# Moving the adaLN modulation sums of a two-layer decoder kernel: from among the routing scores into the pair stage and the last third of routing

## The chip, the cores and the metric

The kernel runs on one core of a Trainium2 chip. The core has five engines, each with an instruction queue of its own: TensorE (PE, with its weight loads as PEld), VectorE (DVE), ScalarE (ACT), GpSimd (POOL) and SyncE (SP), which issues most of the DMA transfers. The metric is the device time of one execution in microseconds; the median of several runs is compared.

## The reference

Two layers work on 512 tokens of width 1024. What matters here is cut out below; `rwkv7_mix` is the recurrent mixer of 8 heads, and the expert layer picks, for each token and head, 16 of 16384 experts by the sums of two 128-way scores.

```python
c_act = jax.nn.silu(c)
for l in range(DEPTH):
    mod = c_act @ ada_w[l] + ada_b[l]                 # 1024 x 6144, one row
    sh1, sc1, g1, sh2, sc2, g2 = jnp.split(mod, 6, axis=-1)
    h = modulate(rmsnorm(x, ln1_g[l]), sh1, sc1)
    ...
    x = x + g1[:, None, :] * mix
    h2 = modulate(rmsnorm(x, ln2_g[l]), sh2, sc2)
    x = x + g2[:, None, :] * peer_ffn(h2, peer_q[l], peer_keys[l], peer_u[l], peer_v[l])
return rmsnorm(x, lnf_g)
```

## The kernel before, in words

The 6144 modulation columns of a layer are done in 12 groups of 512. The groups 0 and 1 are the first shift, 2 and 3 the first scale, 4 and 5 the first gate, 6 and 7 the second shift, 8 and 9 the second scale, 10 and 11 the second gate. A group is a weighted sum of eight 128x512 tiles: `ada_acc` loads them and makes one DVE `tensor_scalar` and seven DVE `scalar_tensor_tensor` on an accumulator `acc`; `ada_mod` then adds up its 128 rows with four one-column matmuls and adds the bias with one small DVE operation. With `early=True` a group is loaded by eight transfers of 256 KB into the general ring `s2` (38 slots), else by four of 512 KB into the ring `raw` (three slots), which the weight loads use as well.

Each layer is a mixer and an expert layer (`peer`).

- **Mixer.** After the input projection the eight heads go in four pairs through blocks (`blocks`, 20 each), a chain of 15 chunk steps (`chain`: a PE product `psc`, then two small DVE operations that give the next state `M`) and an output part. `zipped` deals the blocks of one pair, the chain of the pair before and the output of the one before that evenly; the list `ada` is dealt with them, a third of its entries (`len(ada) // 3`) in each of the first two of these rounds and the rest in the third. Entry i does `ada_mod` of group i-1 and `ada_acc` of group i of `ADA_MIX`. Six groups (4 to 9) give seven entries, so two, two and three.
- **Scoring.** In `peer`, 16 query projections (`project_q`, 24 matmuls each) alternate with `score`: eight matmuls, then `top16` on DVE for four token tiles. From the second projection on, every second one also starts a group of `ADA_PRE` (six in layer 0, two in layer 1), and `ada_mod` comes four projections later.
- **Routing.** A list `main` of weighted steps is dealt by `blend` with the 88 chunks (`s_ahead`, 24 matmuls of 384 columns) whose activations are spilled to memory: first the last score and the picks of token tile 0, then the picks of tile 1, then for t = 1, 2, 3 sixteen `onehot` steps each (four DVE operations, sixteen matmuls), with the picks of tile t+1 between them for t = 1 and 2. The weights (WO = 2.4 for a `onehot`, WP = 2.8 for a pick, and so on) set how many chunks each part gets: `at` splits the 88 chunks over the three parts. Each chunk needs a weight tile split into two halves by ACT (L259) and DVE (L260).
- **Dense.** The 128 chunks are then multiplied by the gates and by the value rows.

The text of the program is in the order told above, and a planner then orders each engine's queue by a simulated timeline. `tc.issue_after(ins)` holds what is traced in its block, on the engine of `ins` alone, behind `ins` in the queue.

Of the kernel before, what the change touches and what calls it, by code (L numbers as in the profile page):

```python
# [15 lines left out]
ALU = mybir.AluOpType  # L16
# [5 lines left out]
NT = T // P  # L22
D = 1024
ND = D // P
L = 2
# [9 lines left out]
SPILL = 88  # L35
GPRE = 24
GFRAC = 0.0
ADA_MIX = [[(l, g) for g in range(4, 10)] for l in range(L)]
ADA_PRE = [[(0, 10), (0, 11), (1, 0), (1, 1), (1, 2), (1, 3)], [(1, 10), (1, 11)]]
ADA_DENSE = [[], []]  # L40
SIDES, NPRE = (0, 8, 0, 3), 2
APER, AOFF, ADEL = 2, 1, 4
# [66 lines left out]
def body(ctx, tc, A, tap=None):  # L109
    nc = tc.nc  # L110
    V, S, G, TE = nc.vector, nc.scalar, nc.gpsimd, nc.tensor
# [11 lines left out]
    def nm(p):  # L123
        cnt[0] += 1
        return f"{p}{cnt[0]}"
# [3 lines left out]
    def bank(shape=(P, T)):  # L129
        return psp[0].tile(list(shape), F32, tag="ps", name=nm("ps"))  # L130

    def sbank(shape=(P, T)):
        return pss.tile(list(shape), F32, tag="pss", name=nm("pss"))

    def s2t(name, shape=(P, T), dt=F32):
        return s2.tile(list(shape), dt, tag="s2", name=nm(name))
# [6 lines left out]
    sc_ = pers.tile([P, ND], F32, name="silu_c")  # L143
# [5 lines left out]
    def C(n):  # L149
        o, w = COFF[n]  # L150
        return const[:, o:o + w]
# [21 lines left out]
    A2 = [pers.tile([P, ND], F32, name=f"A2_{l}") for l in range(L)]  # L173

    first = {}

    def ada_acc(l, g, side=0, early=False):
        acc = s2t("acc")
# [23 lines left out]
    def ada_mod(l, g, acc):  # L202
        pt = sbank((P, 4))
        for m in range(4):
            TE.matmul(pt[:, m:m + 1], acc[:, m * P:(m + 1) * P], C("one"), start=True, stop=True)
        o = VOFF["adab"][0]
        V.tensor_tensor(mods[l][:, 4 * g:4 * g + 4], pt, vecs[l][:, o + 4 * g:o + 4 * g + 4], op=ALU.add)
        if g in (2, 3, 8, 9):
            mod_scale(l, 1 if g < 6 else 2, g % 2)
# [25 lines left out]
    def mod_scale(l, which, half):  # L235
        a, ln, off = (A1, "ln1", 8) if which == 1 else (A2, "ln2", 32)
        o = 4 * half
        V.scalar_tensor_tensor(a[l][:, o:o + 4], mods[l][:, off + o:off + o + 4], 1.0, vec(l, ln, o, 4), op0=ALU.add, op1=ALU.mult)
# [79 lines left out]
    def mixer(l):  # L318
        with ExitStack() as mctx:
# [433 lines left out]

            todo, accs = ADA_MIX[l], {}

# [61 lines left out]
    def peer(l):  # L817
        with ExitStack() as pctx:
# [34 lines left out]
            pace, adas = {}, []  # L853
# [38 lines left out]
            with ExitStack() as rctx:  # L892
# [124 lines left out]
                def onehot(b):  # L1017
                    if not ohr:
                        ohr.extend([[s2t("oh", (P, TB // 2, NK, 2), F16) for _ in range(4)] for _ in range(3)])
                    oj, oi, x1, x2 = ohr[b % 3]  # L1020
                    every = iot.unsqueeze(1).to_broadcast([P, TB // 2, NK, 2])

                    def bc(n):
                        z = sel[n][:, b * TB:(b + 1) * TB].rearrange("p (a b) -> p a b", b=2)
                        return z.unsqueeze(2).to_broadcast([P, TB // 2, NK, 2])

                    V.tensor_tensor(oi, every, bc("i"), op=ALU.is_equal)
                    V.tensor_tensor(x1, oi, bc("g1"), op=ALU.mult)  # L1028
                    V.tensor_tensor(x2, oi, bc("g2"), op=ALU.mult)  # L1029
                    pace["V"] = V.tensor_tensor(oj, every, bc("j"), op=ALU.is_equal)  # L1030
                    onehot_mm()
                    pend.append(b)
# [19 lines left out]

                pre = list(ADA_PRE[l])
                for hp in range(16):
# [13 lines left out]
                def steps(t):  # L1068
                    a, b = route(t)
                    return [(WC, a[0])] + [(WP, f) for f in a[1:-1]] + [(WG, a[-1]), (WT, b)]  # L1070

                steps0 = [(WP, score)] + steps(0)
                steps1 = steps(1)
                main = steps0 + steps1
                for t in range(1, NT):
                    oh = [(WO, lambda b=b: onehot(b)) for b in range((t - 1) * P // TB, t * P // TB)]
                    nx = steps(t + 1) if t + 1 < NT else []
                    for i in range(len(oh)):
                        main.append(oh[i])
                        if nx:  # L1080
                            main.append(nx.pop(0))
                    main += nx
# [18 lines left out]
                w = T // (IG * GB)  # L1101
# [9 lines left out]
            acc = [[bank() for _ in range(2)] for _ in range(NTD)]  # L1111
# [147 lines left out]
    for l in range(L):  # L1259
        mixer(l)  # L1260
        peer(l)
# [56 lines left out]
```

## Time and profile before

| | us |
|---|---|
| median of 3 runs | 3419.54 |
| lowest and highest of them | 3406.15, 3427.21 |
| the profiled execution, its own time | 3418.91 |
| its span in the trace | 3417.1 |

The mean granted TensorE clock of the profiled execution was 0.956 of full speed. In the trace layer 0 has its pair stage at about 230 to 380 us, scoring at 430 to 558, routing at 558 to 985; layer 1 at about 1930 to 2070, 2119 to 2230 and 2230 to 2657. "PE" is matmul time, and a row "a <-b" names who ended a wait. Busy time counts an instruction from its start to its end, so pipelined instructions overlap a little.

### The profile page before, as it was taken

The numbers are of one execution on the slowest core, as the hardware profiler recorded it, in microseconds if no ns is written. First come the engines' busy times: TensorE is split into PE (matmuls) and PEld (weight loads), VectorE is DVE, ScalarE is ACT, GpSimd is POOL, SyncE is SP. The second block draws the span as 40 slices with busy tenths as digits, with TensorE's granted clock in tenths as the row PEclk, the third lists the DMA queues.
The fourth block names the chain that finished last, engine by engine and source line by source line (L and its number), as shares of the span: only waits on it lengthen the run. The fifth ranks groups of instructions, "written<-read, shape, count | busy, mean of one in ns | idle before, by whom it ended". The sixth has DMA issues, their size and how long they took to land. (4 is left out here: it accounts for less than half of the span.)

```text
span 3417.1 us, 52040 instructions
## 1 busy us (share of the span) xinstructions
PE 3187.3 (93%) x18634; PEld 2786.5 (82%) x18634; DVE 2787.6 (82%) x6195; ACT 1396.2 (41%) x2260; POOL 867.6 (25%) x684
## 2 busy tenths in 40 slices
PE   5989898999999999999899898999999999999997
PEld 3777678999998888888777776889999888888886
DVE  5677599989878888899938665999898688888998
ACT  3443222456553343333353433334556433333333
POOL 2000002332212222555400000033240122245664
PEclk7989899999999999999989888999999999999999
DMA  5214343577799999999922233346777999999996
GB/s 197 78 56 153 105 162 122 167 246 258 247 332 348 346 349 315 371 379 371 348 84 81 81 112 124 99 145 197 257 240 278 330 334 343 342 343 345 356 383 251
DMA packets 361380, 826.47 MB, mean 242 GB/s; under 512 B 46496, under 2 KB 189600, under 8 KB 357792
## 3 DMA queue, kind: packets, MB, share of 16 engines
q1 hardware_dynamic: 287392, 554.68, 48.3%
q0 software_dynamic: 73728, 268.47, 20.9%
q8 instruction: 146, 2.39, 0.3%
q14 instruction: 114, 0.93, 0.1%
HBM read 730.75 MB, written 92.27 MB: 241 GB/s over the span
## 5 line engine op out<-in xcount | busy, mean ns | idle before, releaser
L277 PE MATMUL pss<-hi,wsp 128*128 128x384 f32 (+1 forms) x5168 | 1079.9, 360 | 93.0 <-DVE wsp L260 29.1
L1165 PE MATMUL ps<-vv,wg 128*128 128x512 f32 x4608 | 1077.3, 392 | 26.4 <-ACT vv L1148 13.0
L277 PEld LDWEIGHTS pss<-hi,wsp 128*128 128x128 f32 x5168 | 940.0, 195 | 167.7 <-DVE wsp L260 40.2
L1165 PEld LDWEIGHTS ps<-vv,wg 128*128 128x128 f32 x4608 | 867.0, 189 | 210.6 <-ACT vv L1148 17.9
L259 ACT ACTIVATE wsp<-raw 128x1024 fp32r<-128x1024 f32 x341 | 359.9, 1057 | 571.0 <-PE pss L277 403.0
L277 PE MATMUL pss<-lo,wsp 128*128 128x384 f32 (+1 forms) x2584 | 535.3, 347 | 0.0
L858 POOL DMA_INDIRECT row<-u,ex x256 | 313.8, 1226 | 844.1 <-DVE row L864 644.4
L260 DVE TENSOR_TENSOR wsp<-raw,wsp 128x1024 fp32r<-128x1024 f32 x341 | 430.9, 1264 | 76.1 <-ACT wsp L259 75.6
L277 PEld LDWEIGHTS pss<-lo,wsp 128*128 128x128 f32 x2584 | 462.3, 189 | 22.5 <-issue 0.5
L858 POOL DMA_INDIRECT row<-v,ex x256 | 333.6, 1303 | 252.5 <-DVE ox L872 202.9
L1149 DVE TENSOR_TENSOR vv<-raw,vv 128x512 fp32r<-128x512 f32 x512 | 344.2, 689 | 48.8 <-ACT vv L1148 44.1
L1148 ACT ACTIVATE vv<-raw 128x512 fp32r<-128x512 f32 x512 | 291.5, 618 | 120.6 <-DMA raw<-v 83.3
L864 DVE SCALAR_TENSOR_TENSOR row<-row,hx 128x1024 f32<-128x1024 f32 x256 | 318.3, 1249 | 13.3 <-DMA row<-u,ex 13.3
L872 DVE SCALAR_TENSOR_TENSOR ox<-row,wx,ox 128x1024 f32<-128x1024 f32 x254 | 325.2, 1280 | 2.4
L1139 ACT ACTIVATE wg<-ge 128x384 fp32r<-128x384 f32 x256 | 133.0, 524 | 472.4 <-DVE ge L1137 177.2
L974 POOL TENSOR_TENSOR eq<-eq,cid 128x400 f32<-128x400 f32 x128 | 181.7, 1439 | 481.2 <-DVE eq L972 343.0
L940 POOL TENSOR_TENSOR hf<-hi,lo 128x128 f32<-128x128 f32 x16 | 8.1, 526 | 894.8 <-DVE tw L909 868.0
L1140 DVE TENSOR_TENSOR wg<-ge,wg 128x384 fp32r<-128x384 f32 x256 | 141.2, 555 | 108.2 <-ACT wg L1139 97.3
L1049 ACT ACTIVATE gb<-ps 128x512 f32<-128x512 f32 x192 | 199.2, 1163 | 0.0
L1137 DVE TENSOR_TENSOR ge<-ge,g 128x192 f32<-128x192 f32 x496 | 156.8, 353 | 37.1 <-DMA g<-gscr 23.6
L1132 ACT ACTIVATE ge<-pss 128x384 f32<-128x384 f32 x80 | 39.2, 490 | 261.4 <-PE pss L277 259.5
L1028 DVE TENSOR_TENSOR oh<-oh,selg 128x1024 f16<-128x1024 f16 x96 | 71.2, 741 | 46.2 <-PE ps L1047 46.0
(459 smaller groups left out, 3116.7 us busy)
## 6 DMA issues: line engine op xcount, KB each, us to landing
raw<-uT SPq DMA_DIRECT2D x256, 512.0 KB
raw<-v SPq DMA_DIRECT2D x256, 512.0 KB
gscr<-gb SPq DMA_DIRECT2D x24, 2048.0 KB
g<-gscr SPq DMA_DIRECT2D x124, 384.0 KB
gespill<-ge SPq DMA_DIRECT2D x176, 192.0 KB
ge<-gespill SPq DMA_DIRECT2D x176, 192.0 KB
ada<-ada SPq DMA_DIRECT2D x96, 256.0 KB
raw<-ada SPq DMA_DIRECT2D x48, 512.0 KB
```

What stands on the lines that cost most here:

```text
L259: S.activation(w[:, 0], raw, AF.Copy)
L260: V.tensor_tensor(w[:, 1], raw, w[:, 0].bitcast(F32), op=ALU.subtract)
L277: TE.matmul(pt, w[:, a, k * P:(k + 1) * P], hs[k][b], start=start and n == 0, stop=stop and n == len(steps) - 1)
L858: G.indirect_dma_start(out=rows[n], out_offset=None, in_=A["u" if n < P else "v"], in_offset=bass.IndirectOffsetOnAxis(ap=ex[:, n % P:n % ...
L864: V.scalar_tensor_tensor(row, row, 1.0, hx, op0=ALU.mult, op1=ALU.mult, accum_out=dots[:, e:e + 1])
L872: V.scalar_tensor_tensor(ox, row, wx[:, e:e + 1], ox, op0=ALU.mult, op1=ALU.add)
L974: pace["G"] = G.tensor_tensor(eq, eq, z["id"][:, h].unsqueeze(1).to_broadcast([P, 8, NC]), op=ALU.mult)
L1049: S.activation(gb[:, :, o:o + 4].rearrange("p i t -> p t i"), pt, AF.Copy, scale=1.0 / GSC)
L1137: V.tensor_tensor(gq, gq, g[:, :, c % IG], op=ALU.mult)
L1148: S.activation(vv[0][q], raw[:, q * T:(q + 1) * T], AF.Copy)
L1149: vlo[q] = V.tensor_tensor(vv[1][q], raw[:, q * T:(q + 1) * T], vv[0][q].bitcast(F32), op=ALU.subtract)
L1165: end[0] = TE.matmul(acc[t][d2], wg[a][:, ts_], vv[b][d2], start=(c == 0 and a == 0 and b == 0), stop=(c == NK - 1 and a == 1))
```

## The change

`ADA_PRE` becomes empty, so no group is summed among the scores. `ADA_MIX` gets the groups 10 and 11 in each layer: eight groups, nine entries, three in each of the three rounds of the pair stage. The groups 0 to 3 of layer 1 (its first shift and scale) go into layer 0's routing: `ada_parts` cuts each into four steps of two tiles each, with `ada_mod` in the fourth, and the 16 steps follow the 16 `onehot` steps of t = 3, with a weight of 1.3 each. Their DVE operations are held behind the last DVE operation of that `onehot` (`pace["V"]`). They are loaded as the early ones were, by transfers of 256 KB into `s2`.

```diff
-ADA_MIX = [[(l, g) for g in range(4, 10)] for l in range(L)]
-ADA_PRE = [[(0, 10), (0, 11), (1, 0), (1, 1), (1, 2), (1, 3)], [(1, 10), (1, 11)]]
+ADA_MIX = [[(l, g) for g in range(4, 12)] for l in range(L)]
+ADA_PRE = [[], []]
+ADA_LATE = [[(1, g) for g in range(4)], []]
...
+    def ada_parts(l, g):
+        accs = []
+
+        def quarter(q):
+            if q == 0:
+                accs.append(s2t("acc"))
+            for kk in range(2):
+                k = 2 * q + kk
+                w = s2t("ada")
+                nc.sync.dma_start(w, A["ada"][l, g, q, :, kk])
+                if k == 0:
+                    V.tensor_scalar(accs[0], w, sc_[:, k:k + 1], None, op0=ALU.mult)
+                else:
+                    V.scalar_tensor_tensor(accs[0], w, sc_[:, k:k + 1], accs[0], op0=ALU.mult, op1=ALU.add)
+            if q == 3:
+                ada_mod(l, g, accs[0])
+
+        return [lambda q=q: quarter(q) for q in range(4)]
...
+                late = [f for lg in ADA_LATE[l] for f in ada_parts(*lg)]
+
+                def late_step(f):
+                    with tc.issue_after(pace["V"].ins):
+                        f()
+
                 for t in range(1, NT):
...
                     for i in range(len(oh)):
                         main.append(oh[i])
+                        if t == NT - 1 and i < len(late):
+                            main.append((1.3, lambda f=late[i]: late_step(f)))
                         if nx:
                             main.append(nx.pop(0))
```

## Rows read from the trace of the kernel before

**Rows 1.** The page, busy time of each engine over the span.
```profile
PE 3187.3 (93%) x18634; PEld 2786.5 (82%) x18634; DVE 2787.6 (82%) x6195; ACT 1396.2 (41%) x2260; POOL 867.6 (25%) x684
```

**Rows 2.** Windows in both scoring stages: busy us (count) per engine, PEclk, DMA share, GB/s.
```profile
460.00:500.00 40.00, 34.42 (x151) 28.43 (x151) 40.00 (x198) 9.54 (x14) 3.02 (x6) 0.87 0.56 185
500.00:540.00 40.00, 36.00 (x187) 30.66 (x186) 40.00 (x203) 11.57 (x17) 0.00 (x0) 0.96 0.48 158
...
2130.00:2180.00 50.00, 46.41 (x231) 38.89 (x230) 49.45 (x277) 15.31 (x23) 3.82 (x8) 0.97 0.36 116
2180.00:2220.00 40.00, 40.00 (x211) 34.48 (x210) 39.58 (x239) 13.49 (x21) 0.00 (x0) 1.00 0.26 79
```

**Rows 3.** Timeline of ACT: query copies (L919) and the first spilled chunk (L845), both layers.
```profile
429.92 0.60 ACT L919 ACTIVATE qT<-pss 128x512 f32<-128x512 f32 x1 [7.93 <-PE pss L277]
...
544.69 0.58 ACT L919 ACTIVATE qT<-pss 128x512 f32<-128x512 f32 x1
...
558.15 0.87 ACT L845 ACTIVATE ge<-pss 128x384 f32<-128x384 f32 x2
...
2118.89 0.60 ACT L919 ACTIVATE qT<-pss 128x512 f32<-128x512 f32 x1 [8.46 <-PE pss L277]
...
2185.47 0.60 ACT L919 ACTIVATE qT<-pss 128x512 f32<-128x512 f32 x1 [1.87 <-PE pss L277]
...
2191.81 0.60 ACT L919 ACTIVATE qT<-pss 128x512 f32<-128x512 f32 x1 [4.32 <-PE pss L277]
...
2217.25 0.60 ACT L919 ACTIVATE qT<-pss 128x512 f32<-128x512 f32 x1 [4.32 <-issue]
...
2229.70 0.87 ACT L845 ACTIVATE ge<-pss 128x384 f32<-128x384 f32 x2
```

**Rows 4.** Windows in the two pair stages, columns as in Rows 2.
```profile
260.00:270.00 10.00, 7.52 (x81) 6.28 (x80) 9.84 (x22) 4.15 (x10) 0.00 (x0) 1.00 0.57 172
270.00:280.00 10.00, 9.54 (x96) 8.44 (x96) 4.54 (x13) 2.91 (x7) 0.00 (x0) 0.66 0.19 57
...
1960.00:1990.00 30.00, 29.27 (x386) 23.26 (x387) 24.27 (x62) 16.27 (x37) 0.00 (x0) 1.00 0.48 141
```

**Rows 5.** Windows in layer 0's routing and dense stage, columns as in Rows 2.
```profile
558.00:896.00 338.00, 318.55 (x2067) 311.20 (x2068) 310.66 (x801) 160.28 (x202) 120.72 (x84) 0.97 0.66 214
896.00:985.00 89.00, 89.00 (x708) 86.33 (x708) 71.94 (x104) 61.90 (x73) 6.18 (x4) 1.00 0.78 283
...
1000.00:1200.00 200.00, 200.00 (x887) 166.08 (x886) 156.92 (x325) 76.08 (x144) 54.81 (x48) 1.00 1.00 352
```

**Rows 6.** Waits, 860 to 1000 us: total us, times, longest.
```profile
DVE oh L1028 <- PE ps L1047: 18.5, 15, 2.6
```

**Rows 7.** Groups by line, 380 to 570 us: count, busy us, mean ns, idle before.
```profile
L260 DVE TENSOR_TENSOR wsp<-raw,wsp 128x1024 fp32r<-128x1024 f32 x26 | 31.7, 1219 | 6.5 <-ACT wsp L259 6.5
L197 DVE SCALAR_TENSOR_TENSOR acc<-ada,silu_c,acc 128x512 f32<-128x512 f32 x42 | 30.8, 738 | 0.0
```

**Rows 8.** Timeline of PE in layer 0, scoring and the first chunks: start, us.
```profile
518.61 3.89 PE L277 MATMUL pss<-hi,wsp 128*128 128x512 f32 x16
...
524.14 0.94 PE L205 MATMUL pss<-const,acc 128*128 128x1 f32 x8
524.95 1.14 PE L926 MATMUL ps<-keys,qT 128*128 128x128 f32 x8
530.09 5.39 PE L277 MATMUL pss<-hi,wsp 128*128 128x512 f32 x16 [4.00 <-DVE mod L207]
...
562.99 2.93 PE L277 MATMUL pss<-hi,wsp 128*128 128x384 f32 x16
...
567.15 2.93 PE L277 MATMUL pss<-hi,wsp 128*128 128x384 f32 x16
```

**Rows 9.** Waits, 240 to 330 us: total us, times, longest.
```profile
PE psc L709 <- DVE M L711: 5.3, 7, 2.9
```

**Rows 10.** Timeline of PE at the long one of these waits.
```profile
270.46 0.48 PE L709 MATMUL psc<-M,G 64*64 64x64 f32 x4 [2.94 <-DVE M L711]
```

## The prediction

> **What bounds the kernel now.** I read the page first, then the windows stage by stage, then the timeline and the waits at the places that the change touches. The page [rows 1] says that PE is busy for 93% of the span and DVE for 82%. So a DVE operation that goes away pays only where PE waits for DVE, and one that is added costs only where PE comes to wait for it. The windows [rows 2] find such a place: in layer 0's scoring DVE is busy for all 80 us of 460 to 540, while PE has 34.4 and 36.0 of each 40 at granted clocks of 0.87 and 0.96. Layer 1 does the same work with two groups where layer 0 has six, and there PE is full (40.00 of 40, clock 1.00) once the groups are done.
>
> The ACT timeline [rows 3] gives the size. From the first query copy to the first spilled chunk layer 0 takes 558.15 - 429.92 = 128.2 us, layer 1 takes 2229.70 - 2118.89 = 110.8 us. At layer 1's steady pace one projection takes 2191.81 - 2185.47 = 6.34 us, and from its last copy to the first chunk 12.45 us pass; so a stage that PE alone limits would take 15 x 6.34 + 12.45 = 107.6 us.
>
> The pair stage is mixed: DVE has 9.84 of the 10 us from 260, where PE has 7.52 [rows 4]; in layer 1 the load is looser, 24.3 of 30 for DVE and 29.3 for PE. Routing has two halves [rows 5]. From 558 to 896 both engines are nearly full, PE 318.6 and DVE 310.7 of 338 us. From 896 to 985, the sixteen one-hots of t = 3, PE has 89.00 of 89 and DVE 71.9, and DVE's longest-lasting wait is for PE [rows 6]. Only there has DVE room.
>
> **The change part by part.** A group is seven multiply-adds (42 of them are 30.8 us for six groups [rows 7], so 5.1) and one plain multiply, which I put at no more than another 0.74: 5.1 to 5.9 us of DVE. Its four one-column matmuls move PE on by 524.95 - 524.14 = 0.81 us [rows 8].
>
> *Scoring, layer 0.* Six groups leave, 31 to 35 us of DVE and 4.9 of PE. DVE's time alone is not the gain, since PE is then the limit: 128.2 - 107.6 = 20.7 us at most. If the stage comes down only to what layer 1 shows with two groups, it is 128.2 - 110.8 = 17.4. Without sums DVE is still busy for 39.58 of 40 us beside a full PE [rows 2], so the two are then about equal and some waiting between them stays. I take 18.5.
>
> *Scoring, layer 1.* Two groups leave. At most 110.8 - 107.6 = 3.2 us, at least nothing, since DVE's 11 us were largely beside PE's work. I take 2. The 64 loads of the eight groups also leave SP's queue and their slots in the ring `s2`; nothing in the rows waited on them, so I count nothing for it.
>
> *Pair stage.* Two groups more per layer: eight loads of 512 KB on SP through the three `raw` slots, 10 to 12 us of DVE, and 2 x 0.81 = 1.6 us of PE. Nothing is added to the queues of ACT and POOL. The entries become three, three, three; the third round had three already (two groups and a last `ada_mod`), so the added groups lie in the first two rounds. What is queued behind a sum on DVE is the small operation that makes `M`, and PE's next chunk product waits for that with all that is queued on PE behind it. Six groups now go with 5.3 us of such waits [rows 9]; in proportion two more give 1.8, with the matmuls 3.4 us. From below it is the matmuls alone, 1.6 us; a gain is excluded, as nothing is removed there. From above it is the whole DVE time, 11 us per layer, since in places DVE is full already [rows 4]. I take 5 for layer 0, with DVE at 9.84 of 10, and 3.5 for layer 1: 8.5. The loads are covered: the DMA share is 0.57 where the sums are densest.
>
> *The last third of routing.* Four groups: 20 to 24 us of DVE, 32 loads of 256 KB (8.4 MB) and 3.2 us of PE. PE is full there, so the 3.2 us count whole. The DVE time fits: the stretch has 17 us of DVE free, and it grows. The 16 steps weigh 1.3 each, which raises the last part's weight from 174.5 to 195.3 and the total from 236.1 to 256.9. So the 88 chunks are cut at 11 and 21 instead of 12 and 23, and within the last part t = 3 gets 20.4 instead of 14.5 chunks: six chunks leave the earlier steps. A chunk is 567.15 - 562.99 = 4.16 us of PE [rows 8] and 1.22 of DVE [rows 7]. The stretch becomes 89 + 25 + 3.2 = 117 us, with 71.9 + 7.3 + 24 = 103 us of DVE, 88%. I count 1 us for what waits remain (0 to 5). On SP the loads stand ahead of weight loads; the bytes are 283 GB/s x 89 us = 25.2 MB, plus 8.4, plus six chunks of 0.7, 37.8 MB in 117 us or 323 GB/s, and the dense stage sustains 352 beside a full PE [rows 5]. So they are hidden; if that cover failed, at 283 GB/s they would need 134 us, 17 more.
>
> *What the six chunks leave behind.* PE's work from 558 to 896 falls by 25 to 293.6 us, DVE's by 7.3 to 303.4: DVE becomes the longer one. The stretch was 338 us with the longer engine at 318.6, a factor of 1.061. By the same factor it would be 322, 9 us more than the 313 that PE's work alone would give; at DVE full to 97% it is 313, no loss. As layer 0 also starts routing with less scoring work left over on DVE, I take 4.
>
> The sum: -18.5 - 2 + 8.5 + 3.2 + 1 + 4 = -3.8 us. The profiled execution took 3418.9 us (the span and 1.8 around it, which does not change) and lies 0.6 under the median, so the forecast is 3415 us. What the scores give back is largely paid again where the sums go.
>
> **The rivals.** *The pair stage stalls (slower).* The price of one bad place stands in the trace: PE waited 2.94 us for an `M` queued behind sums [rows 10], and the 10 us from 270 then ran at a granted clock of 0.66 [rows 4], a loss of 3.4 more; 6.3 us together, between the two clock levels of 1.2 and 2.4 GHz. The wait of 4.00 us in scoring shows the same: sixteen matmuls took 5.39 instead of 3.89 us after it [rows 8]. Now six groups make one such place in layer 0. If the third group in each of the two rounds makes one more, that is two per layer, 25 us instead of 8.5, and 3432 us. It decides from 12.3 us for both layers on, two such places in all. For it speaks the full DVE at 260 us, against it the looser layer 1.
>
> The Trainium skill speaks for this rival: "TensorE: Matmul & The Clock Gate", section "HAM oscillation — how this bites in real kernels", describes kernels whose matmul bursts restart slowly after each wait for data. By it more waits would cost as above, 3432 us; the trace agrees at the one place, and shows most of the stage at clock 1.00.
>
> *The costs are hidden (more gain).* The pair stage pays only its matmuls, 3.2, the last third 3.2, the shift of chunks nothing, and scoring reaches PE's limit in both layers: -20.7 - 3.2 + 6.4 = -17.5 us, 3401. For it speaks that DVE is at 82% over the span; against it that both engines are full in the earlier parts of routing, which must now run with less PE work beside the same picks.
>
> *The sums do not land where they are written.* Only DVE's queue is held behind the one-hot; if the planner lets the late sums slip past 985 us, they lie in the dense stage beside a full PE with DVE at 157 of 200 [rows 5]. Then the 1 us is saved and the scores gain all the same: 3414, not to be told from the forecast. If instead they crowd the first one-hots of t = 3, PE waits for one-hots, up to the 5 us above: 3419.
>
> **How the numbers follow.** The forecast's own case, with its terms moving by some 10 us around 3415, has 0.55; the pair stage that stalls 0.17; the hidden costs 0.20; the sums that land elsewhere 0.08. The range must reach to 3401 with the runs' own spread (3406 to 3427 for one kernel) and to about 3431: 3398 to 3431. A change of 1%, 34 us, is about what a measurement of this kernel can tell from no change. Faster by that needs more than all of the scoring's gain and some 10 us besides: 0.06. Slower by that needs the stalled pair stage and loads that are not hidden together: 0.05. Within it 0.89.
>
> **What would show it.** In the profile of the changed kernel scoring in layer 0 should take about 110 us from first copy to first chunk with no sums in it, and PE there near full at a clock near 1; layer 1 about 109. In the pair stages PE's waits for `M` should add up to some 7 us instead of 5.3, and a second window with a clock of 0.7 or less would show the first rival. The one-hots of t = 3 should come every 7 us instead of 5.2 with PE full, and the routing before them end some 20 us sooner after its start. The prediction is wrong if scoring stays over 120 us (then DVE alone was not the cause), if PE waits for one-hots at t = 3, or if the pair stages grow by over 20 us together.

## The result and the profile after

The changed kernel takes 3438.24 us (median; 3430.40 to 3448.04) against 3413.80 of the kernel before beside it: a ratio of 1.0059, 95% interval 1.0034 to 1.0085. It is slower by some 20 us, and the time lies above the range of the prediction. The profiled execution has a span of 3432.8 us and an own time of 3434.63, 15.7 above that of [rows 1].

The page after, busy time of each engine: PE has 13.4 us more in 15.7 us more span, for as many matmuls as before.

```profile
PE 3200.7 (93%) x18634; PEld 2803.6 (82%) x18634; DVE 2790.5 (81%) x6195; ACT 1395.2 (41%) x2260; POOL 858.0 (25%) x684
```

The timeline of ACT after, as in [rows 3]: query copies (L939) and spilled chunks (L865) of layer 0, then of layer 1.

```profile
436.54 0.60 ACT L939 ACTIVATE qT<-pss 128x512 f32<-128x512 f32 x1 [8.38 <-PE pss L297]
437.98 0.59 ACT L939 ACTIVATE qT<-pss 128x512 f32<-128x512 f32 x1
444.88 0.58 ACT L939 ACTIVATE qT<-pss 128x512 f32<-128x512 f32 x1
...
527.35 0.60 ACT L939 ACTIVATE qT<-pss 128x512 f32<-128x512 f32 x1 [4.31 <-issue]
...
539.80 0.87 ACT L865 ACTIVATE ge<-pss 128x384 f32<-128x384 f32 x2
...
1009.48 0.49 ACT L865 ACTIVATE ge<-pss 128x384 f32<-128x384 f32 x1 [4.97 <-PE pss L297]
...
2147.08 0.60 ACT L939 ACTIVATE qT<-pss 128x512 f32<-128x512 f32 x1 [7.93 <-PE pss L297]
...
2250.34 0.87 ACT L865 ACTIVATE ge<-pss 128x384 f32<-128x384 f32 x2
```

From first copy to first chunk it is 539.80 - 436.54 = 103.3 us in layer 0 and 2250.34 - 2147.08 = 103.3 in layer 1, where it was 128.2 and 110.8. The last chunk of layer 0 comes 469.7 us after the first; before it came after 436.6, as this row of the kernel before shows with the one in [rows 3].

```profile
994.75 0.49 ACT L845 ACTIVATE ge<-pss 128x384 f32<-128x384 f32 x1 [1.36 <-PE pss L277]
```

The windows after, columns as in [rows 2]: scoring of layer 0 and of layer 1, the answers to [rows 2]; two pieces and the whole pair stage of layer 1, to [rows 4]; routing up to the last sixteen one-hots and from them to the last chunk, to [rows 5].

```profile
440.00:480.00 40.00, 40.00 (x204) 33.95 (x203) 38.21 (x222) 12.81 (x20) 4.96 (x8) 1.00 0.30 93
480.00:530.00 50.00, 50.00 (x259) 42.92 (x258) 49.65 (x298) 16.88 (x25) 0.67 (x1) 1.00 0.27 85
...
2150.00:2200.00 50.00, 50.00 (x252) 42.39 (x251) 48.06 (x280) 16.08 (x26) 5.61 (x8) 1.00 0.31 93
2200.00:2240.00 40.00, 40.00 (x210) 34.39 (x209) 39.65 (x240) 14.15 (x21) 0.00 (x0) 1.00 0.27 82
...
260.00:270.00 10.00, 10.00 (x96) 9.46 (x94) 8.29 (x20) 4.06 (x9) 0.00 (x0) 0.80 0.71 215
270.00:280.00 10.00, 7.52 (x122) 6.44 (x122) 9.47 (x20) 3.44 (x8) 0.00 (x0) 1.00 0.65 202
...
1950.00:2147.00 197.00, 180.25 (x1619) 143.03 (x1616) 133.21 (x289) 66.62 (x136) 0.00 (x0) 0.85 0.39 126
...
540.00:878.00 338.00, 311.76 (x2023) 304.34 (x2024) 304.71 (x781) 161.73 (x200) 105.44 (x83) 0.95 0.63 207
...
878.00:1010.00 132.00, 122.05 (x857) 118.50 (x856) 97.53 (x150) 67.03 (x83) 11.23 (x11) 0.94 0.86 311
```

Both scorings now have a full PE at clock 1.00. In routing it is the last line that is new: where PE had 89.00 of 89 us at clock 1.00 [rows 5], it now has 122.05 of 132 at 0.94, while DVE has 97.53 of 132 and the DMA engines are at 0.86. No engine is full there. The waits of that stretch:

```profile
ACT wsp L279 <- PE pss L297: 51.7, 19, 11.2
DVE wsp L280 <- ACT wsp L279: 13.8, 7, 4.7
DVE acc L191 <- DMA ada<-ada: 13.7, 11, 3.5
...
PE pss L225 <- DVE acc L191: 5.9, 3, 4.5
...
PE ps L1067 <- DVE oh L1050: 3.6, 2, 2.4
```

Cut at the same events in every trace (first chunk product `psc`, first query copy, first and last spilled chunk; within routing the last DVE operation of the first one-hot of t = 1, of t = 2, of t = 3 and of the last one-hot), the two profiled executions stand so, in us:

| stage | before | after | difference | forecast |
|---|---|---|---|---|
| layer 0 to the first `psc` | 239.8 | 242.4 | +2.6 | 0 |
| layer 0 pair stage | 190.1 | 194.1 | +4.0 | +5 |
| layer 0 scoring | 128.2 | 103.3 | -24.9 | -18.5 |
| layer 0 routing to t = 3 | 349.1 | 338.9 | -10.2 | -21 |
| layer 0, sixteen one-hots of t = 3 | 73.2 | 75.9 | +2.7 | |
| layer 0, last one-hot to last chunk | 14.3 | 54.9 | +40.6 | +29.2 with the line above |
| layer 0 dense, layer 1 to its `psc` | 934.7 | 941.0 | +6.3 | 0 |
| layer 1 pair stage | 189.4 | 196.6 | +7.2 | +3.5 |
| layer 1 scoring | 110.8 | 103.3 | -7.5 | -2 |
| layer 1 routing | 436.4 | 432.5 | -3.9 | 0 |
| layer 1 dense to the end | 751.0 | 750.0 | -1.0 | 0 |

The dense stages and the input projections differ by some 10 us between executions whatever the kernel (the second half of layer 0's dense stage took 447 to 469 us in all the traces of this study), so their +6.3 is left unexplained.

Counted where ACT takes a chunk out of its bank, the chunks of layer 0 fall into the five parts first picks, t = 1, t = 2, t = 3, after the last one-hot as 23, 23, 25, 14, 3 before and as 21, 19, 25, 12, 11 after. Six chunks left the earlier parts, as forecast, but t = 3 did not take them: it has fewer than before, and eleven come when no one-hot is left to go beside them.

### The profile page after: what moved, and what is told of

Its sections match the earlier page's. It is cut to its first block, busy times and chain, and to the rows that moved or that the text cites. A ratio compares the mean times of both kernels' runs of the same rounds, so it can differ in the third digit from the quotient of the medians.

```text
span 3432.8 us, 52037 instructions
## 1 busy us (share of the span) xinstructions
PE 3200.7 (93%) x18634; PEld 2803.6 (82%) x18634; DVE 2790.5 (81%) x6195; ACT 1395.2 (41%) x2260; POOL 858.0 (25%) x684
## 5 line engine op out<-in xcount | busy, mean ns | idle before, releaser
L297 PE MATMUL pss<-hi,wsp 128*128 128x384 f32 (+1 forms) x5168 | 1081.7, 360 | 86.5 <-DVE wsp L280 29.2
L884 DVE SCALAR_TENSOR_TENSOR row<-row,hx 128x1024 f32<-128x1024 f32 x256 | 319.1, 1251 | 12.6 <-DMA row<-u,ex 12.6
L994 POOL TENSOR_TENSOR eq<-eq,cid 128x400 f32<-128x400 f32 x128 | 166.6, 1321 | 493.4 <-DVE eq L992 382.9
L960 POOL TENSOR_TENSOR hf<-hi,lo 128x128 f32<-128x128 f32 x16 | 11.2, 728 | 879.6 <-DVE si L931 879.1
L1168 DVE TENSOR_TENSOR wg<-ge,wg 128x384 fp32r<-128x384 f32 x256 | 142.0, 556 | 104.3 <-ACT wg L1167 103.2
L1067 PE MATMUL ps<-oh,oh 128*128 128x128 f16 x1536 | 107.0, 222 | 3.9 <-DVE oh L1050 3.6
```

Of the source, the lines that this page charges most:

```text
L297: TE.matmul(pt, w[:, a, k * P:(k + 1) * P], hs[k][b], start=start and n == 0, stop=stop and n == len(steps) - 1)
L884: V.scalar_tensor_tensor(row, row, 1.0, hx, op0=ALU.mult, op1=ALU.mult, accum_out=dots[:, e:e + 1])
L994: pace["G"] = G.tensor_tensor(eq, eq, z["id"][:, h].unsqueeze(1).to_broadcast([P, 8, NC]), op=ALU.mult)
```

## The experiments

My first theory was the forecast's own weak point: the transfers of the late groups, or DVE's time for them, hold up the one-hots or the weight halves at t = 3. The rivals were the pair stage with its eight groups, the weight of 1.3 that moves chunks, and SP's queue. A last one came up on the way: the four one-column matmuls of a late group (`ada_mod`) take one of only two `pss` banks while their sum still waits for data. (PE writes its products to banks; `pss` is a ring of two of them, `ps` in the expert layer a ring of six.) All numbers of stages below are of layer 0's routing unless they say otherwise; it lasted 436.6 us before and 469.7 after. A stage's length comes from one profiled execution of each kernel; in the eight traces without late groups in it, layer 0's routing took 433.7 to 436.6 us.

### Each half alone

**late_only**: the late groups as in the change, 10 and 11 left among the scores. **mix_only**: the pair stage as in the change, the groups (1, 0 to 3) left among the scores.

```diff
 late_only:
-ADA_MIX = [[(l, g) for g in range(4, 12)] for l in range(L)]
-ADA_PRE = [[], []]
+ADA_MIX = [[(l, g) for g in range(4, 10)] for l in range(L)]
+ADA_PRE = [[(0, 10), (0, 11)], [(1, 10), (1, 11)]]
 mix_only:
-ADA_PRE = [[], []]
-ADA_LATE = [[(1, g) for g in range(4)], []]
+ADA_PRE = [[(1, g) for g in range(4)], []]
+ADA_LATE = [[], []]
```

> Only the late part of the change: the groups 0 to 3 of layer 1 in quarter groups at t = 3 of layer 0's routing; the groups 10 and 11 of each layer are left among the scores, as before. If the loss lies in the last third of routing (theory), layer 0's routing, first to last spilled chunk, stays at about 470 us (436.6 before, 469.7 with the whole change), layer 0's scoring comes to layer 1's length with two groups (about 111 us from first copy to first chunk), the pair stages are unchanged, and the time is 10 to 18 us over the kernel before. If the loss lies in the pair stages (rival), the time is 10 us or more under it.

> Only the other part: groups 10 and 11 of both layers in the pair stage; groups 0 to 3 of layer 1 stay among layer 0's scores. If the loss lies in the last third of routing (theory), layer 0's routing is back at about 437 us, the pair stages keep their 6 to 7 us each, layer 1's scoring its 7.5 us of gain, layer 0's scoring gains 6 to 10, and the time is within 8 us of the kernel before. If the pair stages bear the loss (rival), it is over 10 us slower.

Measured: late_only 3434.39 us, ratio 1.0064 (1.0036 to 1.0091), routing 471.7, scoring 112.4. mix_only 3413.41 us, ratio 1.0003 (0.9981 to 1.0026), routing 434.6, scoring 119.8 and in layer 1 103.3, pair stages 192.9 and 196.9. The loss is the late half. The other half pays what it wins.

### The weight, the loads, the queue, the sums

**late_w0**: the weight of a late step is 0. **late_noload**: the late sums read tiles that are there already. **late_prefetch**: the same loads, issued two steps ahead of their sums. **late_actq**: the loads issued by ACT in place of SP. **late_loadonly**: all loads, but of each group's eight tiles only two are summed.

```diff
 late_w0:
-    main.append((1.3, lambda f=late[i]: late_step(f)))
+    main.append((0.0, lambda f=late[i]: late_step(f)))
 late_noload:
-    w = s2t("ada")
-    nc.sync.dma_start(w, A["ada"][l, g, q, :, kk])
+    w = x[k]
 late_prefetch (ada_load issues the two transfers and appends to ahead):
+    for m in range(3 if n == 0 else n + 2, min(n + 3, 16)) if n else range(3):
+        ada_load(l, m // 4, m % 4)
+    ws = ahead.pop(0)
...
+    w = ws[kk]
 late_actq:
-    nc.sync.dma_start(w, A["ada"][l, g, q, :, kk])
+    nc.scalar.dma_start(w, A["ada"][l, g, q, :, kk])
 late_loadonly:
+    if 0 < k < 7:
+        continue
```

> The whole change, but the 16 late steps weigh 0 instead of 1.3, so that the chunks are cut at 12 and 23 again and none is dealt out of the earlier steps. If the weights are the cause (the first parts of routing have a length that the picks set, whatever chunks lie in them, so chunks taken from them only lengthen the end), layer 0's routing falls from 469.7 to 445 to 455 us. If the late loads in SP's queue are the cause, it stays at 460 or more, as the loads are the same.

> The whole change, but the late sums read resident tiles of x instead of loaded weights: the 32 late loads are left out, so that the first shift and scale of layer 1 come from the wrong data; every DVE and PE operation is there. If the late loads (their place in SP's queue ahead of weight loads, and DVE's 13.7 us of waits for them) are the cause, layer 0's routing falls from 469.7 to about 447 us. If it is the weights of the late steps, it stays at 458 or more; if it is DVE's time for the sums, at 465 or more.

> The whole change, but the two tiles of a quarter group are loaded two steps ahead of its sums instead of just before them; the loads, sums and weights are the same. Layer 0's routing took 469.7 us with the change, 451.0 without the late loads, 436.6 before. If DVE's waits for loads that were issued just before the sums (13.7 us) are what the loads cost, routing falls to 450 to 456 us. If it is the loads' place in SP's queue or the bytes themselves, it stays at 464 or more.

> The whole change, but the 32 late loads are issued from ACT's queue instead of SP's, so that they don't stand between weight loads and spills. If SP's queue order is what the loads cost, layer 0's routing falls from 469.7 to 450 to 456 us. If it is DVE's waits for loads that come just before their use, or the bytes, it stays at 464 or more; ACT's queue then also shows waits of its own.

> The whole change with all 32 late loads, but of each late group only the first and the last tile are summed, so that the first shift and scale of layer 1 are wrong; DVE loses 24 of 32 late operations, about 18 us. If the loads as such (queue and bytes) cost the 19 us, layer 0's routing stays at 462 or more; if the cost is that DVE's sums wait for them with one-hots and weight splits queued behind, it falls to 450 to 457.

| | time, us | ratio to before | routing | t = 3 and after |
|---|---|---|---|---|
| late_w0 | 3427.76 | 1.0042 (1.0018 to 1.0066) | 462.9 | 115.5 |
| late_noload | 3407.41 | 0.9986 (0.9962 to 1.0009) | 451.0 | 113.1 |
| late_prefetch | 3407.87 | 0.9983 (0.9957 to 1.0009) | 451.1 | 112.9 |
| late_actq | 3440.31 | 1.0109 (1.0072 to 1.0146) | 469.5 | 131.5 |
| late_loadonly | 3432.32, one execution | | 469.9 | 131.6 |

Without loads 19 us come back, and as many with every load still there but issued earlier. So the bytes don't cost, only that a sum waits for its tile. Three quarters of the sums' DVE time gone changes nothing, and neither does the issuing queue. The weight is worth 6.8 us of this stage: the chunks are back at 23, 23 and 25 in the earlier parts, and the first part lasts 98 to 100 us with 21 chunks as with 23. But the chunks of t = 3 still fall behind: 7 of the last 17 come after the last one-hot.

### Who suffers from the wait

The timeline of PE after shows what waits with the sum.

```profile
907.01 1.55 PE L297 MATMUL pss<-lo,wsp 128*128 128x384 f32 x8
908.40 4.27 PE L1067 MATMUL ps<-oh,oh 128*128 128x128 f16 x64
915.04 1.20 PE L1067 MATMUL ps<-oh,oh 128*128 128x128 f16 x16 [2.37 <-DVE oh L1050]
917.45 1.89 PE L1067 MATMUL ps<-oh,oh 128*128 128x128 f16 x16 [1.21 <-DVE oh L1050]
919.85 1.87 PE L225 MATMUL pss<-const,acc 128*128 128x1 f32 x8 [0.52 <-DVE acc L191]
921.58 1.63 PE L297 MATMUL pss<-hi,wsp 128*128 128x384 f32 x4
...
978.07 1.84 PE L225 MATMUL pss<-const,acc 128*128 128x1 f32 x8 [4.51 <-DVE acc L191]
979.77 5.03 PE L297 MATMUL pss<-hi,wsp 128*128 128x384 f32 x16
```

From 908.40 on there are six one-hots (four of them in one run of 64 matmuls) and no chunk, until the column sum (L225, eight matmuls in the profile for the four of the program) has been done; then the next chunk starts at once. By the 20 chunks on sixteen one-hots that the weights deal, some seven chunks should have gone beside these six. In these 13 us PE waits for one-hots and for the sum, but for no bank: this is the order in which the planner queued its work. That the planner kept the chunks back for the held bank is a reading of that order, which the next two kernels test. At 978.07 PE itself waits 4.51 us, and the chunk behind it takes 5.03 us for the sixteen matmuls that took 2.93 [rows 8].

Two kernels take this wait from the chunks and leave loads, sums, weights and queue as they are. **late_moddelay**: the column sums of a group come two steps later. **late_psbank**: they stay in their place, but write a bank of the six-slot ring `ps`.

```diff
 late_moddelay:
+    if n in due:
+        ada_mod(*due.pop(n))
     if q == 3:
-        ada_mod(l, g, accs[0])
+        if n == 15:
+            ada_mod(l, g, accs[0])
+        else:
+            due[n + 2] = (l, g, accs[0])
 late_psbank:
-    ada_mod(l, g, accs[0])
+    ada_mod(l, g, accs[0], bank)
...
-    pt = sbank((P, 4))
+    pt = (room or sbank)((P, 4))
```

> The whole change, but the one-column matmuls of each late group (the end of its fourth quarter) come two steps later, except for the very last group; loads, sums and weights are the same. Layer 0's routing took 469.7 us with the change, 469.9 with the loads and only 8 of the 32 sums, 451.1 with loads issued two steps ahead. If the 19 us come from those matmuls, which wait on PE and hold one of the two pss banks until the last sum is done, so that chunks fall behind, routing falls to 450 to 458 us. If it is something else about loads that are issued just before use, it stays at 464 or more.

> The whole change, but the one-column matmuls of the late groups write to a bank of the six of the ps pool instead of one of the two pss banks that the chunks use. If it is the bank that they hold, routing falls from 469.7 to 450 to 458 us. If it is only PE's queue, in order behind a matmul that waits for its sum, it stays at 464 or more.

Measured, one execution each: 3412.45 us with routing 453.7, and 3418.01 with 448.2. (Single executions of the kernel before lie up to 31 us apart here, so it is the stage that counts.) In late_psbank t = 3 takes 19 chunks and four are left for the end; PE's timeline there, and its last chunk:

```profile
910.83 2.93 PE L297 MATMUL pss<-hi,wsp 128*128 128x384 f32 x16
913.60 0.68 PE L297 MATMUL pss<-lo,wsp 128*128 128x384 f32 x3
914.12 0.95 PE L225 MATMUL ps<-const,acc 128*128 128x1 f32 x8
914.93 2.00 PE L1067 MATMUL ps<-oh,oh 128*128 128x128 f16 x32
916.74 1.11 PE L297 MATMUL pss<-lo,wsp 128*128 128x384 f32 x5
...
987.53 0.49 ACT L865 ACTIVATE ge<-pss 128x384 f32<-128x384 f32 x1 [2.72 <-PE pss L297]
```

The column sum goes in between two halves of a chunk, without a wait. The bank by itself gives back 469.7 - 448.2 = 21.5 us, rather more than taking the loads away does. The window of late_psbank over the same stretch, beside the last of the windows after, shows where they went:

```profile
877.00:988.00 111.00, 111.00 (x827) 109.43 (x825) 94.13 (x141) 65.64 (x79) 7.40 (x5) 1.00 0.94 340
```

Here PE is full at clock 1.00. In the changed kernel it has nothing to do for 9.7 of the 130.7 us from the first one-hot of t = 3 to the last chunk, and is busy 10.3 us longer than here for the same 530 chunk matmuls; 1.9 of these are a column sum and sixteen one-hot matmuls that lie outside the stretch here, the rest goes with the clock of 0.94.

Four edits that have nothing in common but to free the chunks from the late sum come to 448 to 454 us; two that leave that tie stay at 470. In the four PE is without work for 0 to 2 us of the stretch, at clock 1.00; in the two for 8 to 11, at 0.92 to 0.94.

### Other places for the sums

**side_score**: the pair stage as in the change, the other four groups among the scores on ACT and POOL in place of DVE. **best1**: prefetch and weight 0, and the groups 10 and 11 in a fourth round of the pair stage, where one chain is left (the first three rounds get two entries each). **best2**: no late groups; these four and the groups 10 and 11 are all in that fourth round of layer 0.

```diff
 side_score (ADA_PRE and ADA_LATE as in mix_only):
-    adas.append((hp, *pre[0], ada_acc(*pre.pop(0), early=True)))
+    adas.append((hp, *pre[0], ada_acc(*pre.pop(0), early=True, side=ND)))
 best1, best2 (and in both the last groups' column sums in a bank of ps):
-    zipped(pt_[3][1], pt_[2][2], fills[FS:FM])
+    zipped(pt_[3][1], pt_[2][2], fills[FS:FM], ada[6:])
 best2:
+ADA_MIX = [[(0, g) for g in range(4, 12)] + [(1, g) for g in range(4)], [(1, g) for g in range(4, 12)]]
```

> Another place for the four groups: they stay among layer 0's scores, as in the kernel that makes only the pair-stage part of the change (layer 0's scoring 119.8 us there), but ACT scales the tiles and GpSimd adds them, so that DVE has none of it. Both are near idle there (ACT 10 of 40 us, GpSimd 3 of 40). If DVE is what the sums cost in scoring, that stage falls to 104 to 107 us and the time is 10 to 16 us under the kernel before; if GpSimd's adds hold up DVE, or ACT's scaling holds up the query copies, it stays at 114 or more.

> The change mended in three places: late loads two steps ahead, late steps with weight 0, and groups 10 and 11 of each layer in the fourth round of the pair stage instead of as a third group in each of the first two. By the stages measured so far: layer 0's scoring 25 us under the kernel before, layer 1's 7.5, layer 0's routing 3 to 12 over it, and the pair stages 0 to 5 over it each instead of some 9: 3388 to 3400 us. If the sums cost the pair stage its 9 us wherever they lie, and the weight makes no difference with early loads, it is 3405 or more.

> No late sums at all: the groups 0 to 3 of layer 1 join 10 and 11 in the fourth round of layer 0's pair stage, where PE's clock is low and DVE half idle; layer 1 as in the mended kernel. If DVE's free time there takes them, layer 0's routing is 437 us, scoring keeps its gains of 25 and 7.5, and the pair stage of layer 0 grows by less than 15: 3390 to 3405 us. If the chain there waits behind the sums, it grows by 25 or more and the time is over 3410.

None of the three came to the time hoped for; each lies on the side of its second reading, best1 and best2 far beyond it. side_score: 3408.48 us, ratio 0.9986 (0.9965 to 1.0006); scoring came from 119.8 only to 116.1. The wait moved to POOL, whose queue now also holds additions, and with it PE:

```profile
494.62 0.47 PE L961 MATMUL ps<-const,hf 128*128 128x128 f32 x1 [4.99 <-POOL hf L960]
```

best1: 3456.27 us, 1.0126 (1.0087 to 1.0166), pair stages 218.1 and 213.4; its routing took 455.9, more than the 451.1 of late_prefetch, which has the same early loads with the weight of 1.3. best2: 3507.90 us, 1.0269 (1.0220 to 1.0319), pair stages 297.2 and 216.5. The timeline of PE and the windows of best2 in that fourth round:

```profile
389.86 1.87 PE L225 MATMUL ps<-const,acc 128*128 128x1 f32 x8 [18.59 <-DVE acc L217]
...
410.33 1.87 PE L225 MATMUL ps<-const,acc 128*128 128x1 f32 x8 [8.59 <-DVE acc L217]
...
430.83 1.87 PE L225 MATMUL ps<-const,acc 128*128 128x1 f32 x8 [12.39 <-DVE acc L217]
```

```profile
350.00:390.00 40.00, 8.05 (x109) 6.51 (x108) 15.00 (x32) 0.00 (x0) 0.00 (x0) 0.57 0.33 104
390.00:430.00 40.00, 10.73 (x54) 7.70 (x54) 15.01 (x34) 1.53 (x3) 0.00 (x0) 0.50 0.34 105
```

With little other work in the round, the column sum stands first in PE's queue and waits for the whole sum, and this for tiles that come at 104 GB/s through the three `raw` slots: 20 us from one column sum to the next. Here a bank of the other ring doesn't help, since PE works its queue in order and the wait is in the queue. In late_psbank it helped because the sum was done by the time the column sum's turn came.

### Why the pair stage grows

In the traces that have the pair stage of the change (twelve in layer 0, eleven in layer 1) it took 192.9 to 201.5 us and 196.2 to 200.7; with seven entries it took 190.0 to 190.1 and 189.4 to 189.9. PE's waits for `M` had not grown, as the row after for [rows 9] shows; over the whole stage they were 7.8 us before and 7.7 after in layer 0, 6.6 and 6.1 in layer 1.

```profile
PE psc L729 <- DVE M L731: 5.0, 7, 2.5
```

Four kernels, all like mix_only otherwise. **mix_sumless** sums only two tiles of the groups 10 and 11; **mix_oneload** loads only two of their tiles; **mix_bank** gives all column sums of the stage a bank of `ps`; **mix_empty** keeps the nine entries and does nothing for these two groups but one small DVE operation each.

```diff
 mix_sumless:
+    if g in (10, 11) and 0 < k < 7:
+        continue
 mix_oneload:
-    nc.sync.dma_start(w, A["ada"][l, g, q])
+    if g < 10 or not q:
+        nc.sync.dma_start(w, A["ada"][l, g, q])
 mix_bank:
-    ada_mod(*todo[i - 1], accs.pop(i - 1))
+    ada_mod(*todo[i - 1], accs.pop(i - 1), bank)
 mix_empty:
-    accs[i] = ada_acc(*todo[i])
+    accs[i] = ada_acc(*todo[i]) if todo[i][1] < 10 else None
```

> Pair stage alone as in mix_only, with all loads of the groups 10 and 11, but only the first and last of the eight tiles of each summed (the second gate comes out wrong; VectorE has 12 operations fewer in each layer's pair stage). If VectorE's time for the added sums is what lengthens the stage, both pair stages are back at 188 to 192 us (mix_only: 192.9 and 196.9) and the clock in them at 0.90. If it is the loads or the new order of the steps, they stay at 193 to 201.

> As mix_only, but of the groups 10 and 11 only the first two tiles are loaded and used for all eight products (the second gate comes out wrong): all VectorE operations of the two groups remain, three quarters of their 4 MB and of their turns in the three-slot ring are gone. If the loads or the ring lengthen the stage, both pair stages are back at 188 to 192 us. If it is VectorE's time or the order, they stay at 193 to 201.

> Pair stage alone as in mix_only, but the column sums of all groups of the pair stage take a bank of the other ring, as the repair of the late groups did. If the held bank lengthens the stage as it did in routing, both pair stages are back at 188 to 192 us and the time is some 10 us under the kernel before. If the other ring is needed as much by the blocks, or the bank is not the cause, they stay at 193 to 201.

> As mix_only, with nine entries dealt three to a round, but the groups 10 and 11 are neither loaded nor summed nor added up (the second gate comes out wrong, one small VectorE operation each stays). If the added work in any form is the cause, both pair stages are back at 188 to 192 us. If the order of nine entries is (three of the six remaining groups in the first round in place of two, and the chains of two pairs meeting otherwise), they stay at 193 to 201.

| | time, us | pair stage, layer 0 | layer 1 |
|---|---|---|---|
| mix_sumless | 3404.59, one execution | 197.3 | 196.9 |
| mix_oneload | 3400.92, one execution | 196.0 | 196.4 |
| mix_bank | 3412.34, ratio 0.9997 (0.9973 to 1.0021) | 201.2 | 203.3 |
| mix_empty | 3417.29, one execution | 196.0 | 195.5 |

Nothing comes back when the sums, the loads or all the work of the groups 10 and 11 are taken out, nor with the other bank: with these two groups empty the stage is still 6 us longer than with seven entries. Layer 1's pair stage as a window, first of the kernel before, then of mix_empty, then of best4 (below), which deals seven entries again:

```profile
1929.00:2119.00 190.00, 173.62 (x1603) 137.22 (x1600) 123.54 (x271) 65.91 (x137) 0.00 (x0) 0.88 0.37 120
```

```profile
1937.00:2133.00 196.00, 178.35 (x1593) 140.56 (x1591) 123.54 (x271) 66.82 (x137) 0.00 (x0) 0.86 0.33 106
```

```profile
1917.00:2108.00 191.00, 172.98 (x1604) 137.43 (x1602) 123.50 (x271) 66.39 (x138) 0.00 (x0) 0.89 0.33 108
```

DVE does 271 operations in the same 123.54 us, and PE much the same matmuls; only PE is busy 4.7 us longer, at a granted clock of 0.86 in place of 0.88. So the dealing is enough: nine entries instead of seven put three of the groups into each of the first two rounds in place of two, and the blocks and chains meet in another order. Which of the two costs is not shown. The groups 10 and 11 lie in the third round, so all four kernels keep the third sum in each of the first two: from the first `psc` to that of the third chain mix_empty has 47 DVE operations on `acc` in each layer, as the changed kernel has, and the kernel before 32. No run deals nine entries with these sums left out.

### Put together

**best3**: the changed kernel with the bank of late_psbank and the weight 0. **best4**: the same, and in layer 1 the groups 10 and 11 leave the pair stage for eight late steps at t = 3 of that layer, so that seven entries are dealt there.

```diff
 best3 and best4: the edits of late_psbank and of late_w0
 best4:
-ADA_MIX = [[(l, g) for g in range(4, 12)] for l in range(L)]
-ADA_LATE = [[(1, g) for g in range(4)], []]
+ADA_MIX = [[(0, g) for g in range(4, 12)], [(1, g) for g in range(4, 10)]]
+ADA_LATE = [[(1, g) for g in range(4)], [(1, 10), (1, 11)]]
```

> The changed kernel with both repairs of the late groups: their column sums take a bank of the other ring, and their weight is 0, so that the chunks keep the shares of the kernel before. If the bank and the weight are the two causes and independent, layer 0's routing ends at 441 to 446 us (448.2 with the bank alone, less up to 6.8 for the weight), and the time is some 10 us under the kernel before: scoring -25 and -7.5, pair stages +8 each, routing +7 and -3, ratio 0.996 to 0.999. If the weight's gain and the bank's are the same microseconds, routing stays at 447 to 450 and the ratio is 0.998 to 1.001.

> The same, and in layer 1 the groups 10 and 11 leave the pair stage for eight quarter steps at t=3 of that layer's own routing. If a pair stage with eight groups costs 8 us and a repaired late group costs at most 2 us, layer 1's pair stage is back at 189 to 191 us, its scoring stays at 103 and its routing grows from 432 to 434 to 437: some 4 to 6 us under the other kernel, ratio to the kernel before 0.994 to 0.998. If late groups cost what they cost in layer 0 (about 3 us each after the repair), the two are equal.

best3: 3400.49 us, ratio 0.9969 (0.9954 to 0.9984), routing 446.2, between the two readings: beside the bank the weight gave 2.0 us in place of 6.8, which is within the spread of this stage. best4: 3387.46 us, ratio 0.9951 (0.9929 to 0.9974), the best of all; layer 1's pair stage is back at 189.9 us from 199.6, and its routing is 438.7 where the kernels without late groups there had 428.9 to 436.4. Not all of that is the two groups' doing: from the first one-hot of t = 3 to the last chunk, where they lie, it is 89.0 us in place of 87.5, so they cost 1.5 together, as the first reading had it (at most 2 each), and the rest lies before them. In the pair stage 9.7 us are saved. Its profiled execution also has a short dense stage in layer 1 (452.3 us in its second half, 463.6 to 479.2 elsewhere), which nothing in the edit explains. Over twelve executions each, the ratios put it 6 us under best3, the means 9 (95% interval 1 to 17).

## Why the prediction was wrong

**What bounds the kernel.** Right: DVE limited the scoring stages, and without sums PE is full there at clock 1.00.

**The scoring terms, -18.5 and -2, were too small; the step that failed is the floor of 107.6 us.** It took fifteen paces of 6.34. After the change the paces are 6.38, but the first two copies are 1.44 us apart (436.54 and 437.98), since two projections are ready when the first copy starts; so it is 1.44 + 14 x 6.38 + 12.45 = 103.2 us. Both layers reach it. The short first pace could have been read before: this row of the kernel before is the second copy, 1.44 us after the first of [rows 3], and layer 1 has the same 1.44.

```profile
431.36 0.59 ACT L919 ACTIVATE qT<-pss 128x512 f32<-128x512 f32 x1
```

The waiting between the two nearly equal engines, for which I kept 2 us in layer 0 and 1 in layer 1, did not come: DVE is busy for 38.21 of 40 and 49.65 of 50 us and PE has lost nothing. The stage gave 24.9 and 7.5, together 11.9 more than forecast.

**The last third of routing: the step "I count 1 us for what waits remain" failed.** The stretch from the first one-hot of t = 3 to the last chunk grew by 43.3 us, not by 29.2. Its premise was sound as far as it went: the bytes fit (0.86 of the DMA engines, 311 GB/s) and DVE had room. But a transfer that fits in the mean can still land after its consumer is due: the late sums waited eleven times for a tile issued just before (13.7 us in all), and the column sum behind it held one of two banks through which all chunks go. The forecast counted DVE's time, PE's and the bytes there, and no buffer that a late sum takes; the thing held was a bank. PE did wait for one-hots, for 3.6 us, which the forecast named as a sign that it was wrong; yet the sixteen took 75.9 us in place of 73.2, where it expected 7 us each, and it was the chunks that stayed behind. With another bank the stretch grows by 23.0 (110.5 from 87.5 us), 6.2 less than forecast. That is all PE's work: 128 chunk matmuls more (5.3 chunks, 22.2 us at 4.16 each) and three column sums (2.4), less 21 one-hot matmuls (1.4) that lie elsewhere.

**The chunks moved: "PE's work from 558 to 896 falls by 25", less 4, failed in size.** 10.2 us came, not 21, though 128 chunk matmuls or 22.2 us of PE's work did leave. The first part of routing lasts 98 to 100 us with 21 or 23 chunks, so what was taken out there (50 matmuls, 8.7 us) gave nothing: PE is busy for 87.2 of its 99.5 us, where it was for 92.7 of 99.3, and DVE for 88.0, so neither is full. What sets that length is not shown. The 78 matmuls taken out of t = 1, 13.5 us, gave 10.9. So a chunk gave back its 4.16 us of PE only in part where PE was not full, and cost them in full at t = 3, where PE was.

**The pair stage: +8.5 forecast, +11.2 in this execution, some 15 over all that share it (6.2 and 8.7 by their means).** The place and the sign were right, and the size came nearer than its mechanism deserved, by luck: PE's waits for `M`, from which the term was made, went from 5.3 to 5.0 us instead of 7, and what grew was PE's busy time at a lower clock (layer 1: 173.62 us at 0.88 before, 180.25 at 0.85 after). mix_empty shows the stage 6 us longer without the work of the groups 10 and 11; whether the sums that now come earlier or the order is the price stays open. The first rival named this stage, and its 25 us were not reached. The one window that it was built on, at clock 0.66, is gone (0.80 and 1.00 stand there now), and two of its places at 6.3 us would have been 12.6, not 12.3.

The sum of the forecast's own terms at their measured sizes: scoring -32.4, pair stages +11.2, routing of layer 0 +33.1, is +11.9 us, and the stages that were counted at nothing add +4.0: the 15.7 of the spans, to the roundings. The range failed with one term, routing, whose bounds of 0 to 5 and 0 to 9 us were drawn round how much DVE and the DMA engines can do, where the cause was when a load was issued and which bank waited for it.

The Trainium skill has a sentence for the cause that was found: "Perfetto Trace Analysis", section "Matmuls", says that independent matmul groups should rotate through different PSUM banks, so that one is emptied while the next is computed. late_psbank agrees for routing, 469.7 to 448.2 us. mix_bank shows no gain in the pair stage: with the same move of ring it took 201.2 and 203.3 us, near and above the top of the spreads given above, and the kernel's time is that of mix_only (3412.34 and 3413.41 us). And the Trainium skill, "TensorE: Matmul & The Clock Gate", section "HAM oscillation — how this bites in real kernels", tells of matmul bursts that start slowly again after each wait for data. The trace agrees where the wait was long: after 4.51 us idle, sixteen matmuls took 5.03 us in place of 2.93, and a column sum took 1.84 and 1.87 us where late_psbank has 0.95.

## What to carry to other kernels

Of work that is moved beside a full engine, follow every buffer that it takes as well as its time: an accumulator bank of a two-slot ring, taken by an operation whose data are only just being loaded, stops what shares the ring, however small the operation; load some steps ahead, or use a ring that has room. An order dealt evenly from a list changes with the list's length, so the price of two more entries need not be that of their own work: run the entries empty before their work is made cheaper, and remember that the other entries have moved too. And work that leaves an engine gives its time back only where that engine was full: here 22.2 us of PE's work gave 10.2 where it left, and cost all of it where it went.

## What the runs showed of the hardware

The granted clock of a stretch can fall, and TensorE's busy time grow, with nearly the same work dealt in another way: 173.62 us at 0.88 and 178.35 us at 0.86 for layer 1's pair stage, with 271 DVE operations in 123.54 us in both. With a bank held, routing's last third had 9.7 us without work on TensorE and some 8 us more at a clock of 0.94, where the same matmuls went at 1.00 with another bank. Eight one-column matmuls took 0.95 us where the clock was 1.00 and 1.87 where it was 0.50 to 0.57, the two levels of 2.4 and 1.2 GHz. In the fourth round of best2, with PE busy for 8 to 11 of 40 us, the clock stayed at 0.50 to 0.57 for 80 us. And the DMA engines moved 311 GB/s in the stretch that lost most, with tiles that still came too late: what counted was when a load was issued, not how much was moved.
